# High and low halves of attention's output stored to two DRAM tensors, added there later by four DMAs; the third copy of q one tick later

## Chip, cores and metric

The kernel runs on one core of a Trainium2 chip. The metric is the device time of one execution in microseconds (us), lower is better. The engines are PE (TensorE, matmuls), ACT (ScalarE), DVE (VectorE), POOL (GpSimd) and SP (SyncE, which here only issues DMAs); sixteen DMA engines move data. DMAs that add to what they write (accumulating DMAs) are all issued by POOL in this kernel.

## What is computed

One decoder layer over 512 tokens and a width of 2048, float32. Attention is cut here to what the change touches:

```python
h = rms_norm(x, norm_gain[i])
z = h @ w_in[i]
q, k, v, g_attn, c_b, c_c, c_h, g_conv = jnp.split(z, SPLITS, axis=-1)
q = partial_rope(rms_norm(q, q_norm_gain[i]), pos)      # 16 heads of 64
k = partial_rope(rms_norm(k, k_norm_gain[i]), pos)      # 4 heads of 64
y_attn = sliding_window_attention(q, k, v, attn_sinks[i]) * jax.nn.silu(g_attn)   # window 128
y_conv = c_b * short_conv(c_c * c_h, conv_w[i]) * jax.nn.silu(g_conv)             # 3 taps
mix = jnp.concatenate([y_attn, y_conv], axis=-1)
x = x + mix @ w_out[i]
gate = jax.nn.sigmoid(rms_norm(x, ple_gate_norm_gain[i]) @ w_ple_gate[i] + b_ple_gate[i])
e = rms_norm(p[i] @ w_ple_proj[i], ple_norm_gain[i])
x = x + gate * e
```

## The kernel before

**Precision.** Every float32 operand of a matmul is split into a high part, which a cast rounds to PE's format, and a low part, the rest (`halves`, line 199 the cast on ACT, line 200 the subtraction on DVE). A product is three matmuls: high by high, low by high, high by low.

**Stages.** First the keys and values are projected (line 520). Then come nine *groups* of a Strassen-like product, groups 0 to 8, of 28 *steps* each; a step is 12 matmuls of 128x512 (line 241). Group 0 gives q. Between group 0 and group 1 stands the *attention stage*: it computes attention itself, together with the tiles of the convolution's input (`gemm_tile`, line 712) and the embedding's projection (line 900). Groups 1 to 3 go on with the convolution (`square_group`, `conv_group`), group 4 gates attention's output, groups 5 and 6 are the output projection, 7 and 8 the gate.

**What sets the order.** PE's order is written out by hand everywhere. In the groups the order of all other engines is by hand too: `soon(before, s, ...)` and `soon(after, s, ...)` enter work into tables that step s empties. In the attention stage only PE's is: there a scheduler orders ACT, DVE, SP and POOL, from the order in which the program issues the work and its own estimates. Each engine runs its own list in order and waits where an operand isn't there. The stage's program order is made of *ticks*: every six matmuls of `gemm_tile` call `tick`, which issues all that was entered by `at(when, ...)` up to that tick.

**Attention.** Sixteen *units* (j, n): key head j, in the order 2, 3, 0, 1, and block n of 128 queries. For a pair of blocks, `turn_q` (five ticks before the unit's scores) transposes q into PSUM (line 791), splits it into `st` and `low`, and builds the two tiles that the scores need with three copies of half a tile each, DMAs from SBUF to SBUF that POOL issues: line 795 `st2` upper half from `st`, 796 `st2` lower half from `low`, 797 `st` lower half from `low`. The third overwrites what the first reads, so it waits until the first has landed.

Per unit then: scores on PE (`pss`, lines 814 and 815), masking and maximum on DVE (823 to 831), four exponentials on ACT (line 833, tile `prob`); four ticks later `turn`: PE transposes `prob` (line 842, `pst`), ACT and DVE split it into `pth` and `ptl`, and POOL makes masked copies `pph` and `ppl` (line 849, affine select) of it; three ticks after that `values`: four matmuls into `pso` (line 859) with `pth`, `ptl`, `pph`, `ppl` in this order. The values' high and low parts lie side by side in the weights, so the upper 64 rows of the result `up` (line 861) are the high part's and the lower 64 the low part's; their sum is the output. The kernel forms that sum in DRAM: line 863 stores the upper half into `attn_dram[j]` (the tile `a`), and line 864, entered twelve ticks after the scores, adds the lower half with an accumulating DMA. That one reads and writes what 863 wrote, so POOL waits ahead of it until 863 has landed.

```python
rows = attn_dram[j].rearrange("(r d) (n t) -> d r n t", d=HD, n=NB)[:, :, n]
nc.gpsimd.dma_start(rows, up[:HD])
cell["add"] = lambda: nc.gpsimd.dma_start(rows, up[HD:], accum_op=ALU.add)
```

**After attention.** `attn_dram` is read in group 4 (line 1132, `load_raw`), from step 18 of that group on. Group 1's *taps* (line 1055 on DVE, its store line 1056 on POOL, tile `t`) run into the first steps of group 2: six products of the tile `z` with a row, each stored to DRAM. The fifth tap's product goes to the buffer from which the fourth tap's store still reads, so DVE waits for that store. POOL also issues the accumulating DMAs of the weights' sums (line 169, tile `wy`).

Of the kernel before, what the change touches and what calls it, by code (L numbers as in the profile page):

```python
# [9 lines left out]
F32 = mybir.dt.float32  # L10
F32R = mybir.dt.float32r
AF = mybir.ActivationFunctionType
ALU = mybir.AluOpType
E = mybir.EngineType

P = 128
T = 512
D = 2048
KT = D // P
NB = T // P  # L20
HD = 64
NH = 16
NKV = 4
# [12 lines left out]
def hymba_layer(ctx: ExitStack, tc: tile.TileContext, io):  # L36
# [14 lines left out]
    nc = tc.nc  # L51
# [5 lines left out]
    dram = ctx.enter_context(tc.tile_pool(name="dram", bufs=1, space=bass.MemoryType.DRAM))  # L57
# [54 lines left out]
    PER = len(steps) // NG  # L112
# [4 lines left out]
    before, after = {}, {}  # L117

    def soon(table, s, fn, *args):
        table.setdefault(s, []).append((fn, args))  # L120
# [3 lines left out]
    for g in range(NG):  # L124
        w, n = groups[g]
# [72 lines left out]
    def halves(h, l, src):  # L198
        nc.scalar.copy(h, src)  # L199
        tt(l, src, f32(h), op=ALU.subtract)  # L200
# [90 lines left out]
    def h_slot(home):  # L291
        return home, home_pool(home).tile([P, 2, 2 * P], F32R, tag=home, name="form")
# [44 lines left out]
        soon(before, s0 + 21, lambda: join(qs[1, 1], g, "a", ALU.subtract))  # L337
        soon(after, s0 + 26, lambda: join(qs[0, 0], g, "c", ALU.add))

    attn_dram = [dram.tile([2 * P, T], F32, name=f"a{j}") for j in range(NKV)]  # L340
    conv_dram = [dram.tile([P, T], F32, name=f"c{i}") for i in range(4)]
    mix_dram = [dram.tile([P, T], F32, name=f"m{i}") for i in range(8)]
    tap_dram = [dram.tile([T, T], F32, name=f"t{i}") for i in range(3)]
# [339 lines left out]
    def mtile(name):  # L683
        return misc.tile([P, T], F32, tag="m", name=name)
# [5 lines left out]
    def at(when, fn):  # L690
        later.append((when, len(later), fn))
# [91 lines left out]
    def turn_q(j, t):  # L783


        pt = ps_m.tile([P, T], F32, name="psm")
        for b in range(2):
            for f in range(2):
                s = j % 2 * 2 * P + f * P
                i = 2 * b + f  # L790
                nc.tensor.transpose(pt[:, i * P : (i + 1) * P], qs[t, j // 2][:, b, s : s + P], ident)
        st, st2 = (rowp.tile([P, T], F32R, tag="rows", name="st") for _ in range(2))
        low = misc.tile([P, T], F32R, tag="m", name="low")
        halves(st, low, pt)
        nc.gpsimd.dma_start(st2[:HD], st[HD:])
        nc.gpsimd.dma_start(st2[HD:], low[HD:])
        nc.gpsimd.dma_start(st[HD:], low[:HD])
        turned[j, t, 0], turned[j, t, 1] = st, st2

    turned = {}  # L800

    def attention(j, n, when):

        lo = 0 if n else P
        cell = {}
# [49 lines left out]
        def values():  # L855
            po = ps_o.tile([P, 4, P], F32, name="pso")
            for i, (w, x) in enumerate(cell["pt"]):
                w = w.rearrange("p s d -> p (s d)")
                nc.tensor.matmul(po, w, x, start=i == 0, stop=i == len(cell["pt"]) - 1)  # L859
            up = mtile("up").rearrange("p (r t) -> p r t", t=P)  # L860
            nc.scalar.copy(up, po)
            rows = attn_dram[j].rearrange("(r d) (n t) -> d r n t", d=HD, n=NB)[:, :, n]
            nc.gpsimd.dma_start(rows, up[:HD])
            cell["add"] = lambda: nc.gpsimd.dma_start(rows, up[HD:], accum_op=ALU.add)

        if n % 2 == 0:
            at(when - 5, lambda: turn_q(j, n // 2))
        at(when, scores)
        at(when + 4, turn)
        at(when + 7, values)  # L870
        at(when + 12, lambda: cell["add"]())


    pgs = []
# [31 lines left out]
    for u, (j, n) in enumerate(order):  # L906
        attention(j, n, 13 + 35 * u // 15)
# [101 lines left out]
    def new_pair(into, j, move=False):  # L1009
        raw = [spare("raw") for _ in range(2)]  # L1010
        into[j], work = make_forms(raw, lambda: spare("g"), form_slot, drop=let_go, move=(lambda: itile("g")) if move else None)
        pairs[id(into), j] = raw, work
# [116 lines left out]
    def load_raw(j, src):  # L1129
        new_pair(mixf, j, move=j == 4)  # L1130
        for i in range(2):
            nc.sync.dma_start(pairs[id(mixf), j][0][i], src[(2 * j + i) % 8])

    attn_tiles = [attn_dram[i // 2][i % 2 * P : (i % 2 + 1) * P] for i in range(8)]

    def attn_group(g):
# [24 lines left out]
        for j, when, plan in (  # L1161
# [4 lines left out]
        ):  # L1166
            soon(after, s0 + when, load_raw, j, mix_dram)
            for s, names in plan.items():
                soon(after, s0 + s, pieces, mixf, j, names)
# [266 lines left out]
    low = h_slot("fx")  # L1436
# [88 lines left out]
def build(arrays):  # L1525
    import concourse.bacc as bacc

    nc = bacc.Bacc("TRN2", target_bir_lowering=False, num_devices=1)
    io = {
        n: nc.dram_tensor(f"in_{n}", v.shape, mybir.dt.from_np(v.dtype), kind="ExternalInput").ap()  # L1530
        for n, v in arrays.items()
    }
    io["out"] = nc.dram_tensor("out_t", (NB, P, D), F32, kind="ExternalOutput").ap()
    with tile.TileContext(nc) as tc:
        hymba_layer(tc, io)
    return nc
# [9 lines left out]
```

## Time and profile before

| | |
|---|---|
| Runs shown (three) | 913.33, 914.39, 915.92 us; median 914.39 |
| The profiled execution | 912.85 us; its span, first to last instruction, 911.1 us |
| PE busy | 900.5 us, 99% of the span; granted clock 0.998 |
| DVE, ACT, POOL busy | 714.1, 527.7, 193.0 us (78%, 58%, 21%) |
| Attention stage | from about 127 to 280 us of the span |
| Groups 1 and 2 | from 280 to about 433 us |

All times below are us from the start of the span. A row of the timeline gives start, duration, engine, line, operation, its tiles as out<-in, and in brackets how long the engine was idle ahead of it and what ended the wait. A matmul's duration is its latency; PE starts one of 128x512 every 0.23 us, so back-to-back rows start 0.23 apart. A DMA's row on POOL is its issue; the transfer lands later. A wait that no engine on the path feels costs nothing: POOL is idle for most of the span.

### The profile page before, as it was taken

What the parts mean: (1) busy time and instruction counts of PE and PEld (TensorE: products, weight loads), DVE (VectorE), ACT (ScalarE), POOL (GpSimd) and SP (SyncE); (2) the same over time, 40 slices, a digit from 0 to 9 for tenths busy, and PEclk for the clock granted to TensorE, in tenths of its full rate; (3) what the DMA queues carried; (4) which work ended last, traced back from release to release, by engine and by line L of the source; (5) the groups of instructions that cost most, each with busy time, mean ns of one, the idle gap of its engine ahead of it and who ended that gap; (6) DMA issues with size and microseconds to landing.
All of it is one profiled execution on the core that took longest, in us unless ns stands there. A gap on an engine that the chain in (4) does not pass through costs nothing.

```text
span 911.1 us, 11967 instructions
## 1 busy us (share of the span) xinstructions
PE 900.5 (99%) x4130; PEld 746.3 (82%) x4130; DVE 714.1 (78%) x967; ACT 527.7 (58%) x849; POOL 193.0 (21%) x264
## 2 busy tenths in 40 slices
PE   9999999999999999999999999999999999999997
PEld 7888888887878888888888888888888888888885
DVE  6878889887757687877768678997858887799678
ACT  6766848676653443454344457766556666665453
POOL 4232143376640001100130110012120112111100
PEclk9999999999999999999999999999999999999999
DMA  8999558756668858648478897858996995898647
GB/s 312 360 292 308 212 61 274 246 112 133 151 130 310 288 173 237 179 147 257 126 201 247 222 237 257 234 127 230 341 293 198 212 293 142 234 306 256 185 139 219
DMA packets 74445, 202.34 MB, mean 222 GB/s; under 512 B 8867, under 2 KB 15331, under 8 KB 74384
## 3 DMA queue, kind: packets, MB, share of 16 engines
q1 hardware_dynamic: 48672, 134.24, 43.1%
q0 software_dynamic: 25568, 67.33, 33.0%
q8 instruction: 32, 0.52, 0.2%
q14 instruction: 29, 0.24, 0.1%
q10 hardware_dynamic: 144, 0.01, 0.0%
HBM read 166.94 MB, written 31.46 MB: 218 GB/s over the span
## 4 chain that ended last, share of the span: by engine, by line
PE 86%; DVE 5%; issue 2%; ACT 2%; DMA 2%; POOL 2%; SPq 0%; DVEq 0%; POOLq 0%; ACTq 0%
PE psp L241 68%; PE psg L712 4%; PE pst L241 4%; PE psp L520 3%; PE pst L1024 2%; PE pss L900 1%; PE pst L1422 1%; PE pst L900 1%; DMA raw<-in_w_kv 1%; DVE wl L200 1%; DVE z L1320 1%; PE pso L859 1%; DMA st<-st 1%; DVE ptl L200 0%; DMA a<-up 0%
## 5 line engine op out<-in xcount | busy, mean ns | idle before, releaser
L241 PE MATMUL psp<-wh,form 128*128 128x512 f32 x1280 | 395.3, 390 | 0.0
L241 PEld LDWEIGHTS psp<-wh,form 128*128 128x128 f32 x1280 | 239.4, 188 | 49.2
L241 PE MATMUL psp<-wl,form 128*128 128x512 f32 x640 | 249.4, 390 | 0.0
L200 DVE TENSOR_TENSOR wl<-wy,wh 128x1024 fp32r<-128x1024 f32 x108 | 131.5, 1221 | 58.6 <-ACT wh L199 57.9
L199 ACT CAST wh<-wy 128x1024 fp32r<-128x1024 f32 x108 | 113.4, 1051 | 91.6 <-PE psp L241 72.4
L241 PEld LDWEIGHTS psp<-wl,form 128*128 128x128 f32 x640 | 120.1, 188 | 25.8 <-DVE wl L200 0.8
L200 DVE TENSOR_TENSOR wl<-wx,wh 128x1024 fp32r<-128x1024 f32 x72 | 87.9, 1222 | 51.2 <-ACT wh L199 51.1
L199 ACT CAST wh<-ws 128x1024 fp32r<-128x1024 f32 x72 | 75.8, 1053 | 74.0 <-PE psp L241 53.0
L241 PE MATMUL psp<-wh,hsh 128*128 128x512 f32 x304 | 118.6, 390 | 0.0
L241 PE MATMUL psp<-wl,hsh 128*128 128x512 f32 x304 | 118.3, 389 | 0.0
L241 PE MATMUL psp<-wh,hsl 128*128 128x512 f32 x304 | 118.3, 389 | 0.0
L199 ACT CAST wh<-wx 128x1024 fp32r<-128x1024 f32 x72 | 75.6, 1052 | 70.9 <-PE psp L241 49.9
L200 DVE TENSOR_TENSOR wl<-ws,wh 128x1024 fp32r<-128x1024 f32 x72 | 88.0, 1222 | 29.2 <-ACT wh L199 28.9
L189 DVE TENSOR_TENSOR wy<-wy,ws 128x1024 f32<-128x1024 f32 x72 | 87.6, 1217 | 0.0
L241 PEld LDWEIGHTS psp<-wl,hsh 128*128 128x128 f32 x304 | 57.1, 188 | 11.9
L241 PEld LDWEIGHTS psp<-wh,hsl 128*128 128x128 f32 x304 | 57.1, 188 | 11.8
L241 PEld LDWEIGHTS psp<-wh,hsh 128*128 128x128 f32 x304 | 57.1, 188 | 11.7
L712 PE MATMUL psg<-hsh,wh 128*128 128x512 f32 x112 | 45.3, 405 | 0.0
L712 PE MATMUL psg<-hsh,wl 128*128 128x512 f32 x112 | 43.8, 391 | 0.0
L712 PE MATMUL psg<-hsl,wh 128*128 128x512 f32 x112 | 43.8, 391 | 0.0
L169 POOL DMA_DIRECT2D wy<-in_w_mid x16 | 14.0, 876 | 136.9 <-DVE wy L189 83.3
L199 ACT CAST wh<-raw 128x1024 fp32r<-128x1024 f32 (+1 forms) x29 | 29.1, 1005 | 19.7 <-DMA raw<-in_w_ple_proj 6.9
(236 smaller groups left out, 1332.1 us busy)
## 6 DMA issues: line engine op xcount, KB each, us to landing
ws<-in_w_mid SPq DMA_DIRECT2D x40, 512.0 KB, 4.5
wx<-in_w_mid SPq DMA_DIRECT2D x24, 512.0 KB, 4.4
wy<-in_w_mid SPq DMA_DIRECT2D x20, 512.0 KB, 6.1
h<-form POOLq DMA_DIRECT2D x32, 256.0 KB, 5.7
wy<-in_w_mid POOLq DMA_DIRECT2D x16, 512.0 KB, 8.8
raw<-in_w_in SPq DMA_DIRECT2D x16, 512.0 KB, 4.6
wx<-in_w_out SPq DMA_DIRECT2D x16, 512.0 KB, 6.7
ws<-in_w_out SPq DMA_DIRECT2D x16, 512.0 KB, 6.2
```

The costliest lines, as they stand in the source:

```text
L169: nc.gpsimd.dma_start(t, w[n, r, j, c], accum_op=ALU.add)
L189: tt(y, y, got[g, "s1" if f == 6 else "s0", c], op=ALU.add)
L199: nc.scalar.copy(h, src)
L200: tt(l, src, f32(h), op=ALU.subtract)
L241: nc.tensor.matmul(ps[t], a, w[:, i], start=start and first and i == 0 and n == 0, stop=last and i == 1 and n == 2, skip_group_check=not s ...
L520: nc.tensor.matmul(kv_ps[t // 2][:, t % 2], hs[k][a][:, t * P : (t + 1) * P], kv_split[c][w][:, i], start=k == 0 and n == 0, stop=k == KT ...
L712: nc.tensor.matmul(ps, w[:, k % 8], a, start=k == 0 and n == 0, stop=k == KT - 1 and n == 2)
L859: nc.tensor.matmul(po, w, x, start=i == 0, stop=i == len(cell["pt"]) - 1)
L900: nc.tensor.matmul(banks[t], a, w[:, k], start=k == 0 and i == 0, stop=k == 1 and i == 2)
L1024: nc.tensor.transpose(pt[:, b], quads[b // 2][:, b % 2, f * P : (f + 1) * P], ident)
L1320: stt(z[:, b, cols], z[:, b, cols], column(r_e, t, b), ext[t, n][b][:, cols], op0=ALU.mult, op1=ALU.mult)
L1422: nc.tensor.matmul(ps, w[:, k % 8], a, start=k == 0 and n == 0, stop=k == KT - 1 and n == 2)
```

## The change

- `low_dram` is new: four DRAM tensors `l`, shaped as `attn_dram`. `values` issues two plain stores in a row (both on line 864 now), the upper half of `up` to `a`, the lower half to `l`. The sixteen accumulating DMAs of line 864 and their entries at `when + 12` are gone.
- `add_low` (line 1135) adds the whole of `low_dram[j]`, 512 KB, to `attn_dram[j]` with one accumulating DMA from DRAM to DRAM, in rows of 128 numbers. The four are entered after steps 4, 9, 14 and 19 of group 2.
- `turn_q` returns its third copy (now line 798) in place of issuing it; it is entered one tick later, at `when - 4`.

```diff
-    attn_dram = [dram.tile([2 * P, T], F32, name=f"a{j}") for j in range(NKV)]
+    attn_dram, low_dram = ([dram.tile([2 * P, T], F32, name=f"{x}{j}") for j in range(NKV)] for x in "al")
...
         nc.gpsimd.dma_start(st2[:HD], st[HD:])
         nc.gpsimd.dma_start(st2[HD:], low[HD:])
-        nc.gpsimd.dma_start(st[HD:], low[:HD])
         turned[j, t, 0], turned[j, t, 1] = st, st2
+        return lambda: nc.gpsimd.dma_start(st[HD:], low[:HD])
...
-            rows = attn_dram[j].rearrange("(r d) (n t) -> d r n t", d=HD, n=NB)[:, :, n]
-            nc.gpsimd.dma_start(rows, up[:HD])
-            cell["add"] = lambda: nc.gpsimd.dma_start(rows, up[HD:], accum_op=ALU.add)
+            for i, x in enumerate((attn_dram, low_dram)):
+                rows = x[j].rearrange("(r d) (n t) -> d r n t", d=HD, n=NB)[:, :, n]
+                nc.gpsimd.dma_start(rows, up[i * HD : (i + 1) * HD])
 
         if n % 2 == 0:
-            at(when - 5, lambda: turn_q(j, n // 2))
+            at(when - 5, lambda: cell.update(last=turn_q(j, n // 2)))
+            at(when - 4, lambda: cell["last"]())
         at(when, scores)
         at(when + 4, turn)
         at(when + 7, values)
-        at(when + 12, lambda: cell["add"]())
...
+    def add_low(j):
+        nc.gpsimd.dma_start(attn_dram[j], low_dram[j], accum_op=ALU.add, max_dma_last_dim=T)
+
+    for j in range(NKV):
+        soon(after, 2 * PER + 4 + 5 * j, add_low, j)
```

The lists of PE, DVE, ACT and SP hold the same instructions in the same order as before; only POOL's differs, from the 69th instruction on. Three places of it follow; a row is line, operation and tiles.

The first place is on POOL about the middle of the attention stage, from the three copies for units (0, 0) and (0, 1) on. Before:

```order
L795 DMA st<-st 64x512
L796 DMA st<-low 64x512
L797 DMA st<-low 64x512
L863 DMA a_85<-up 64x4x128
L849 AFFINE_SELECT pph<-pth 128x512
L864 DMA a_85<-up 64x4x128
L849 AFFINE_SELECT ppl<-ptl 128x512
L863 DMA a_86<-up 64x4x128
```

The same place of POOL's list in the change:

```order
L795 DMA st<-st 64x512
L796 DMA st<-low 64x512
L798 DMA st<-low 64x512
L864 DMA a_85<-up 64x4x128
L864 DMA l_89<-up 64x4x128
L849 AFFINE_SELECT pph<-pth 128x512
L864 DMA a_86<-up 64x4x128
L849 AFFINE_SELECT ppl<-ptl 128x512
```

Between `pph` and `ppl` stood an accumulating store that waits for the store two rows above it; now a plain store of the next unit stands there, and the pair of stores comes ahead of `pph`. The third copy stands where it stood, directly behind the other two.

The second place is on POOL at the end of the attention stage, the last units (1, 2) and (1, 3) and the first accumulating DMAs of group 1. Before:

```order
L849 AFFINE_SELECT pph<-pth 128x512
L863 DMA a_84<-up 64x4x128
L849 AFFINE_SELECT ppl<-ptl 128x512
L864 DMA a_84<-up 64x4x128
L863 DMA a_84<-up 64x4x128
L849 AFFINE_SELECT pph<-pth 128x512
L849 AFFINE_SELECT ppl<-ptl 128x512
```

In the change:

```order
L849 AFFINE_SELECT pph<-pth 128x512
L864 DMA a_84<-up 64x4x128
L849 AFFINE_SELECT ppl<-ptl 128x512
L864 DMA l_88<-up 64x4x128
L864 DMA a_84<-up 64x4x128
L864 DMA l_88<-up 64x4x128
L849 AFFINE_SELECT pph<-pth 128x512
```

Ahead of the last `pph` there was one accumulating store and one plain one; now there are three plain ones, none of which waits for another's landing.

The third place is on POOL in groups 1 and 2, the taps' stores (line 1056). One piece of the difference, from the third tap's store on, before and in the change:

```order
L1056 DMA t_99<-z 128x2x512
L1056 DMA t_101<-z 128x2x512
L1056 DMA t_100<-z 128x2x512
L1056 DMA t_99<-z 128x2x512
L169 DMA wy<-in_w_mid 128x1024 x4
```

```order
L1056 DMA t_103<-z 128x2x512
L1135 DMA a_83<-l_87 1024x128
L1056 DMA t_105<-z 128x2x512
L1056 DMA t_104<-z 128x2x512
L1135 DMA a_84<-l_88 1024x128
L1056 DMA t_103<-z 128x2x512
L1135 DMA a_85<-l_89 1024x128
L1135 DMA a_86<-l_90 1024x128
L169 DMA wy<-in_w_mid 128x1024 x4
```

The first addition stands ahead of the fourth tap's store, the second ahead of the sixth, and the last two behind the sixth, ahead of group 3's weight sums. Each waits on POOL only for the stores of the attention stage, so it is issued when POOL reaches it.

## The prediction

> **What bounds the kernel now.** I read the page first, then the busy time by stage, then PE's waits, then POOL's groups in the attention stage, and at the waits the timelines of PE, POOL, ACT and DVE.
>
> ```profile
> span 911.1 us, 11967 instructions
> PE 900.5 (99%) x4130; PEld 746.3 (82%) x4130; DVE 714.1 (78%) x967; ACT 527.7 (58%) x849; POOL 193.0 (21%) x264
> ...
> 270.00:560.00 290.00, 290.00 (x1297) 240.39 (x1296) 215.15 (x206) 132.69 (x141) 32.11 (x41) 1.00 0.74 219
> ```
>
> PE is idle for 911.1 - 900.5 = 10.6 us of the span, and in groups 1 to 3 (the third row, 270 to 560 us) for none. The change adds no matmul and takes none away, so all that it can win is idle time of PE, and all that it can lose is new idle time. PE's waits by releaser tell how much of it the touched instructions cause:
>
> ```profile
> PE pso L859 <- POOL ppl L849: 1.8, 1, 1.8
> ...
> PE pso L859 <- POOL pph L849: 0.6, 1, 0.6
> PE pss L814 <- DMA st<-low: 0.4, 1, 0.4
> ```
>
> Three waits, all in the attention stage, 2.8 us: for `ppl`, for `pph`, and for the third copy of q. Against this stand POOL's own waits there (the groups of 166 to 290 us; after the bar busy time, mean ns, then idle time and its releasers):
>
> ```profile
> L864 POOL DMA_DIRECT2D a<-up x16 | 17.0, 1089 | 25.6 <-DMA a<-up 24.3 <-PE pss L815 1.4
> ...
> L797 POOL DMA_DIRECT2D st<-low x7 | 4.3, 617 | 8.1 <-DMA st<-st 7.2 <-DVE rope L413 0.7 <-issue 0.2
> ```
>
> POOL waits 24.3 us in all for a store ahead of the accumulating stores that follow it. These are gone with the change, but they are not the gain: POOL is off the path, and PE feels two of them. The gain is read at those two.
>
> **First place: `ppl` at 211.** POOL's rows, DVE's for `ptl`, and PE's (unit (3, 1)):
>
> ```profile
> 205.64 0.65 POOL L863 DMA_DIRECT2D a<-up  x1
> 206.29 0.66 POOL L849 TENSOR_SCALAR_AFFINE_SELECT pph<-pth 128x512 fp32r<-128x512 f32 x1
> 209.82 1.06 POOL L864 DMA_DIRECT2D a<-up  x1 [2.87 <-DMA a<-up]
> 210.49 1.05 POOL L849 TENSOR_SCALAR_AFFINE_SELECT ppl<-ptl 128x512 fp32r<-128x512 f32 x1
> ...
> 205.97 0.69 DVE L200 TENSOR_TENSOR ptl<-pst,pth 128x512 fp32r<-128x512 f32 x1
> ...
> 209.43 0.39 PE L859 MATMUL pso<-pph,vd 128*128 128x512 f32 x1
> 211.59 0.50 PE L859 MATMUL pso<-ppl,vd 128*128 128x512 f32 x1 [1.78 <-POOL ppl L849]
> ```
>
> `ptl` is there at 206.66, but `ppl` stands behind the accumulating store, which waits for the landing of the store at 205.64, and ends at 211.54. PE would have come to it at 209.43 + 0.23 = 209.66 and starts at 211.59: **1.93 us** lost. In the change two plain stores of 0.65 stand ahead of `pph` and one between `pph` and `ppl`. Even if the third copy again goes out as late as before (it ends at 205.64 there), `pph` ends at 205.64 + 2 x 0.65 + 0.66 = 207.6 and `ppl` at 207.6 + 0.65 + 0.66 = 208.9, ahead of 209.66. The wait goes whole.
>
> What is late next? PE goes on to the transposes of (3, 2), whose last exponential is long done (first row), so it runs on. ACT and DVE can't follow at once: ACT is in the exponentials of (3, 3), which depend on scores from before the wait, until 210.66 + 0.48 = 211.14, and after those come the copy `up` and `pth`:
>
> ```profile
> 207.66 0.48 ACT L833 ACTIVATE prob<-prob,negms,msq 128x128 f32<-128x128 f32 x1
> 210.66 0.48 ACT L833 ACTIVATE prob<-prob,negms,msq 128x128 f32<-128x128 f32 x1
> 212.62 0.59 ACT L199 CAST pth<-pst 128x512 fp32r<-128x512 f32 x1
> ...
> 213.50 0.69 DVE L200 TENSOR_TENSOR ptl<-pst,pth 128x512 fp32r<-128x512 f32 x1
> ...
> 231.87 0.48 ACT L833 ACTIVATE prob<-prob,negms,msq 128x128 f32<-128x128 f32 x1
> ...
> 233.43 0.60 PE L791 MATMUL psm<-ident,z 128*128 128x128 f32 x4
> ...
> 184.59 0.48 ACT L833 ACTIVATE prob<-prob,negms,msq 128x128 f32<-128x128 f32 x1
> ...
> 185.30 0.48 PE L712 MATMUL psg<-hsh,wh 128*128 128x512 f32 x1
> ```
>
> So `pth` moves from 212.62 to 211.14 + 0.1 + 0.48 (the copy) = about 211.7, and `ptl`, which waits for it, from 213.50 to 211.7 + 0.59 + 0.05 = 212.35: DVE moves by 1.15 us, not by 1.93. I let DVE keep that lag (a gap in its work would shorten it). The first place where the lag could reach PE is the transposes of (0, 2): their last exponential ends at 231.87 + 0.48 = 232.35, and PE's next work begins at 233.43. At 184.6 PE did wait for exponentials, and went on 185.30 - (184.59 + 0.48) = 0.23 us after the last. Moved by 1.15, the exponentials let PE go on at 232.35 - 1.15 + 0.23 = 231.43; PE, moved by 1.93, comes at 231.50. It fits by 0.07 us: this place lets through 2.0 us and no more. Of the first gain I take 1.93.
>
> **The third copy.** PE's wait for it is worth 0.4 us in the row above. In the change it still stands directly behind the first two and still waits for the first one's landing; what it is spared is queueing behind accumulating stores. It comes ahead of `pph` now, which has 0.8 us to spare by the sum above. If its 0.4 us goes, it goes before the place that lets 2.0 through, so it is worth at most 2.0 - 1.93 = 0.07. I take 0; the ends are 0 and 0.4.
>
> **Second place: the last unit.** POOL, PE, ACT and DVE:
>
> ```profile
> 264.34 1.06 POOL L864 DMA_DIRECT2D a<-up  x1 [3.83 <-DMA a<-up]
> ...
> 265.76 0.39 PE L859 MATMUL pso<-ptl,vv 128*128 128x512 f32 x1
> 266.75 0.49 PE L859 MATMUL pso<-pph,vd 128*128 128x512 f32 x1 [0.60 <-POOL pph L849]
> ...
> 267.67 0.40 PE L712 MATMUL psg<-hsh,wh 128*128 128x512 f32 x1
> ...
> 262.04 0.58 ACT L861 COPY up<-pso 128x512 f32<-128x512 f32 x1
> 262.52 0.58 ACT L199 CAST pth<-pst 128x512 fp32r<-128x512 f32 x1
> ...
> 263.31 0.68 DVE L200 TENSOR_TENSOR ptl<-pst,pth 128x512 fp32r<-128x512 f32 x1
> ```
>
> Without a wait PE reaches its next tile at 265.76 + 3 x 0.23 = 266.45; it does so at 267.67: **1.22 us** lost, since `pph` and `ppl` stand behind a store that waited 3.83 us. In the change `pph` has two plain stores ahead of it that need `up` (262.62) and nothing else: 262.62 + 1.3 + 0.66 = 264.6, `ppl` 265.2, where PE wants them at 265.99 and 266.22. All four engines move together here, for the chain of this unit starts at PE's scores, so the distance holds. Nothing is late next: PE goes on with matmuls whose operands are loaded.
>
> **The four additions.** They take no time of PE, ACT or DVE. The size that matters is D, the time the DMA engines need for one. From 211.25 to 212.45 (1.2 us) one accumulating store of 512-byte rows has the engines to itself; the other rows are the page's 512 KB accumulations into SBUF and 128 KB stores of `up`, the taps' stores, two rows of DVE, and a piece of the chain that ended last:
>
> ```profile
> q0 software_dynamic: 230, 0.12, 100.3%
> ...
> wy<-in_w_mid POOLq DMA_DIRECT2D x16, 512.0 KB, 8.8
> ...
> a<-up POOLq DMA_DIRECT2D x32, 128.0 KB, 3.4
> ...
> DMA to landing us min/median/max: 3.2/3.8/7.4
> ...
> 365.96 0.75 POOL L1056 DMA_DIRECT2D t<-z  x1 [0.61 <-DVE z L1055]
> 373.18 0.75 POOL L1056 DMA_DIRECT2D t<-z  x1 [6.46 <-DVE z L1055]
> ...
> 381.19 1.22 DVE L1055 TENSOR_TENSOR z<-z,tap 128x1024 f32<-128x1024 f32 x1
> ...
> 385.73 1.22 DVE L200 TENSOR_TENSOR wl<-wy,wh 128x1024 fp32r<-128x1024 f32 x1
> ...
> 280.09 160.48 PE psp L241 x708
> ```
>
> One packet takes 16 x 1.2 x 1.003 / 230 = 84 ns of an engine. An addition is 1024 packets of that size, 64 for each engine: D = 5.4 us. No row shows DRAM to DRAM. Above I bound it by the 8.8 us in which a 512 KB accumulation from DRAM lands, waits included; below by the 3.2 us of a plain 512 KB store (the row of `t`, which gives 3.2 to 7.4). I take 5.4, the row of the same packet size.
>
> Behind the first addition on POOL's queue stands the fourth tap's store, issued at 373.18; for that store waits DVE's fifth tap, 381.19; behind it on DVE stand the splits of weights. The third tap's store, the slowest of the six, lands at 365.96 + 7.4 = 373.4. The addition follows in the same queue, then the fourth store with about 1.6 us of its own: it lands at 373.4 + D + 1.6 = 380.4, ahead of 381.19. If it is later, PE feels nothing until the split at 385.73 is 2.4 us late: it feeds step 12 of group 2, which starts 40 steps of 160.48 / 59 = 2.72 us after 280.09, at 388.9, and its third matmul needs the low part 0.45 later; the split ends at 386.95. So PE waits only from D = 381.19 - 375.0 + 2.4 = **8.6 us** on, then one for one; at the upper bound 0.2 us. The other three additions have the weights of later steps beside them and only the sixth tap's store behind them, which no engine waits for soon. POOL spends at least 1.06 us (256 rows) and at most 4 times that on issuing one: between the third store's issue and 373.18 it has 6.5 us idle. In the attention stage it saves 0.4 us for each of sixteen stores (1.06 against 0.65).
>
> A rule speaks against this. The row of DMA traffic for 366 to 379 us:
>
> ```profile
> q1 hardware_dynamic: 9, 0.04, 1.5%
> ```
>
> The queue of the weight loads takes 1.5% of the engines there. By the Trainium skill, DMA: Bandwidth & Descriptors, section Queues, rings and completion order, each DMA engine takes turns between the queues that have work. By that rule a full weight queue would leave an addition half of each engine, and the time would be that of rival 5; by the row there is next to nothing to take turns with at the first addition, and the sum stays. The trace so far shows no addition beside a full weight queue.
>
> **Sum.** 1.93 + 0 + 1.22 = 3.15 us. The profiled execution took 912.85 us, 1.75 more than its span, so it becomes 909.7. It lies 1.54 below the median of the runs shown, 914.39; the time I predict is the median's, 914.39 - 3.15 = **911.2 us**, faster by 0.34%. About 0.3%, 2.7 us, is what a measurement of this kernel can tell from no change.
>
> **Rivals.**
> 1. *The exponentials take the wait's place.* If ACT and DVE don't move at all after 211, PE can pass (0, 2) only 0.23 after 232.35, at 232.58 in place of 233.43: 0.85 us of the first gain is left, 0.85 + 1.22 = 2.07, 912.3 us. For it: a fit by 0.07 us is no margin. Against: `pth` and `ptl` have only the copy ahead of them.
> 2. *All three waits go whole*, 0.4 + 1.93 + 1.22 = 3.55: 910.8 us. Against it stands the 2.0 at (0, 2).
> 3. *The change doesn't unblock POOL.* The third copy, 7.2 us of waits, now stands ahead of `pph`; if its landing wait grows by over 0.8 us, `ppl` is late again and only the last unit gains: 1.22, 913.2 us. For it: the order. Against: fewer slow stores in the queue.
> 4. *Slower: the first addition holds the fourth tap's store.* If rows from DRAM to DRAM cost much more than 84 ns, DVE stands at the fifth tap and PE runs dry at step 12. It decides from D = 8.6; the gain is eaten at D = 8.6 + 3.15 = 11.75. With each quarter taking the whole 3.4 us in which such a 128 KB store lands (the page's median), D = 13.6, a loss of 5.0: 916.2 us; at twice that, 930.
> 5. *The first addition shares the engines with weight loads.* If loads came as it runs and each queue had half, D would be 2 x 5.4 = 10.8, a loss of 2.2: 913.4 us. Against: the 1.5%.
>
> **How the numbers follow.** Forecast 0.50, rival 1 0.21, rival 2 0.08, rival 3 0.07, rival 4 0.11, rival 5 0.03. Faster by over 0.3% means below 911.65. Runs of one kernel lie about 1 us apart, so of the forecast seven in ten fall there, all of rival 2 and a tenth of rival 1: 0.35 + 0.08 + 0.02 = 0.45. Rival 4 lies beyond +0.3% in most of its span: 0.09. The rest, 0.46, is within. The range takes in the forecast, rivals 1 to 3 and 5, the bounds of D and half a us of the runs' spread on either side: 910.0 to 914.2; rival 4 is left out.
>
> **What would show it.** Right: POOL's groups have no wait for `a<-up`; PE's waits for `ppl` and `pph` are gone; the transposes of (0, 2) start without a wait or with one under 0.3 us; idle time of PE in the attention stage near 0; an addition lands within 9 us and DVE's fifth tap has no wait. Wrong: a wait of `pst` for `prob` near 1 us (rival 1); `ppl` still a releaser of PE (rival 3); the fifth tap waiting for `t<-z` and PE idle in group 2 (rival 4). The forecast also falls if PE turns out to be paced by something hidden in its modelled ends.

## The result, and the profile after

| | Runs | Median (lowest to highest), us | Ratio to before, 95% interval |
|---|---|---|---|
| before | 6 | 914.66 (912.13 to 915.92) | |
| changed | 6 | **909.65** (909.37 to 910.13) | 0.9949 (0.9935 to 0.9964) |
| before, a second set | 29 | 913.83 (911.40 to 916.49) | |
| changed, the same set | 12 | 910.13 (909.46 to 914.04) | 0.9961 (0.9946 to 0.9975) |

The ratios, which are those of the means, make the kernel faster by 3.6 to 4.7 us; the medians lie 5.0 and 3.7 us apart. The changed kernel's runs lie closer together: all of its eighteen but one are within 1.5 us. The profiled execution went from 912.85 to 909.53 us, by 3.32.

The head of the page after:

```profile
span 907.8 us, 11971 instructions
...
PE 898.9 (99%) x4130; PEld 746.0 (82%) x4130; DVE 714.2 (79%) x967; ACT 527.7 (58%) x849; POOL 193.0 (21%) x268
```

The row of groups 1 to 3 in its busy times by stage:

```profile
270.00:560.00 290.00, 290.00 (x1297) 240.44 (x1296) 216.76 (x209) 135.45 (x147) 36.18 (x43) 1.00 0.79 226
```

PE is idle for 8.9 us in place of 10.6, and in groups 1 to 3, where the additions run, still for none. PE's waits by releaser have one row of the attention stage left, and POOL's groups there have no wait for a landing of `a`:

```profile
PE pso L859 <- POOL ppl L849: 0.6, 1, 0.6
```

```profile
L864 POOL DMA_DIRECT2D a<-up x16 | 10.2, 637 | 17.9 <-ACT up L861 16.7 <-issue 1.0
L864 POOL DMA_DIRECT2D l<-up x16 | 10.1, 631 | 1.1 <-issue 1.1
...
L798 POOL DMA_DIRECT2D st<-low x7 | 3.7, 527 | 6.5 <-DMA st<-st 6.5
```

The first place, POOL and then PE:

```profile
205.99 0.62 POOL L864 DMA_DIRECT2D a<-up  x1
206.61 0.65 POOL L849 TENSOR_SCALAR_AFFINE_SELECT ppl<-ptl 128x512 fp32r<-128x512 f32 x1
...
208.80 0.39 PE L859 MATMUL pso<-pph,vd 128*128 128x512 f32 x1
209.03 0.39 PE L859 MATMUL pso<-ppl,vd 128*128 128x512 f32 x1
```

`ppl` ends at 207.26, 1.8 us ahead of its matmul, which follows the one before it by 0.23. The second place reads the same: the four matmuls of the last `pso` start 0.23 apart and the next tile 0.23 behind them. What is left is at unit (0, 2). POOL, DVE and PE there:

```profile
231.07 0.65 POOL L864 DMA_DIRECT2D l<-up  x1 [1.07 <-issue]
231.73 0.65 POOL L849 TENSOR_SCALAR_AFFINE_SELECT pph<-pth 128x512 fp32r<-128x512 f32 x1
232.32 1.71 POOL L849 TENSOR_SCALAR_AFFINE_SELECT ppl<-ptl 128x512 fp32r<-128x512 f32 x1
...
232.33 1.21 DVE L200 TENSOR_TENSOR wl<-raw,wh 128x1024 fp32r<-128x1024 f32 x1
...
234.08 0.50 PE L859 MATMUL pso<-ppl,vd 128*128 128x512 f32 x1 [0.63 <-POOL ppl L849]
```

`ppl` took 1.71 us here in place of 0.65, beside a split of weights on DVE, and PE lost time that it did not lose before. The two other profiles with the same order here (`changed_again`, `no_additions`) have the same 1.71.

Set against the same matmuls of before, PE is 0.7 us earlier by 100 us (ahead of anything that the change touches), gains 0.57 at the third copy, gives back 0.66 at the transposes of (3, 1) right behind it, gains 2.0 at the first place, gives back 0.9 at (0, 2), gains 1.2 at the last unit, and 0.3 at the end. The attention stage gives 2.3 of the 3.3 us.

The additions, POOL's rows and DVE's fifth tap:

```profile
361.70 0.75 POOL L1056 DMA_DIRECT2D t<-z  x1 [0.62 <-DVE z L1055]
362.44 1.41 POOL L1135 DMA_DIRECT2D a<-l  x1
368.86 0.79 POOL L1056 DMA_DIRECT2D t<-z  x1 [5.01 <-DVE z L1055]
...
378.17 1.22 DVE L1055 TENSOR_TENSOR z<-z,tap 128x1024 f32<-128x1024 f32 x1
```

The issue of an addition takes 1.4 us. The first one lands 11.3 us after its issue began, 4.0 us behind the third tap's store ahead of it, and the fifth tap does not wait.

### The profile page after: what moved, and what is told of

Its sections match the earlier page's. It is cut to its first block, busy times and chain, and to the rows that moved or that the text cites. A ratio compares the mean times of both kernels' runs of the same rounds, so it can differ in the third digit from the quotient of the medians.

```text
span 907.8 us, 11971 instructions
## 1 busy us (share of the span) xinstructions
PE 898.9 (99%) x4130; PEld 746.0 (82%) x4130; DVE 714.2 (79%) x967; ACT 527.7 (58%) x849; POOL 193.0 (21%) x268
## 4 chain that ended last, share of the span: by engine, by line
PE 72%; DVE 3%; ACT 2%; issue 1%; DMA 1%; POOL 0%; DVEq 0%; ACTq 0%; POOLq 0%
PE psp L241 60%; PE psg L712 4%; PE pst L241 4%; PE pst L1024 2%; PE pst L1428 1%; PE pso L859 1%; ACT prob L833 1%; DVE z L1326 1%; DVE wl L200 0%; PE pst L842 0%; DMA wx<-in_w_out 0%; PE pss L815 0%; PE pss L814 0%; DMA st<-st 0%; DVE wy L189 0%
## 5 line engine op out<-in xcount | busy, mean ns | idle before, releaser
L833 ACT ACTIVATE prob<-prob,negms,msq 128x128 f32<-128x128 f32 x64 | 30.8, 483 | 16.9 <-DVE negms L831 16.9
```

Source lines behind the costliest of these rows:

```text
L833: nc.scalar.activation(t[:, r], t[:, r], AF.Exp, scale=r_q[:, r : r + 1], bias=negm[:, r : r + 1], accum_out=sums[:, r : r + 1],)
```

## The experiments

Two things had to be explained: how the change gains more than the one profile of before showed as waits, and why the runs of before lie so far apart. In a diff, `...` marks lines left out. "Lists" are the instructions of each engine in order.

### Parts of the change

**Only the third copy later** (`copy_only`).

```diff
-        nc.gpsimd.dma_start(st[HD:], low[:HD])
         turned[j, t, 0], turned[j, t, 1] = st, st2
+        return lambda: nc.gpsimd.dma_start(st[HD:], low[:HD])
...
-            at(when - 5, lambda: turn_q(j, n // 2))
+            at(when - 5, lambda: cell.update(last=turn_q(j, n // 2)))
+            at(when - 4, lambda: cell["last"]())
```

> The kernel before with only the third copy entered a tick later. The lists of all five engines hold the same instructions in the same order as before, so this is also a second look at the kernel before. Every theory: ratio 1.000 within 0.002, runs between 912 and 916 us. Its profile is a second execution to read: if it lies above 914 us (the profile of before lay at 912.85), the place where it is later than that profile names the loss that the median of before has and its profile doesn't show. Theory A (landings of the accumulating stores vary, POOL hands the delay to pph and ppl): more than three PE waits for pph or ppl, in the attention stage. Theory B (the weight loads for group 1 wait for the buffers from which the last accumulating stores read): PE idle at 280 to 295 us. Theory C (launch, head or tail): PE's starts differ before 127 us or after 820 us.

914.86 us (911.42 to 919.32, 12 runs), ratio 1.0012 (0.9991 to 1.0032): no effect that shows. The profile, at 911.42 us, has the same lists as before and no wait at 211. So the wait that carried most of my sum is not a property of the program: it comes in some executions.

**The changed kernel without that edit** (`split_copy_early`): the two hunks above undone in the changed kernel.

> The changed kernel with the third copy issued in the program where it was before. In the lists one low store of POOL changes places with the affine select behind it, nothing else. All theories: the time of the changed kernel, 909.6 us within 0.5; the tick of the third copy has no part in the gain. Rival: the copy's tick is worth the 0.4 us that PE waited for it: 910.0.

910.32 us (909.68 to 913.47, 9 runs), ratio 0.9956 (0.9940 to 0.9972). The median is 0.2 to 0.3 us above both forecasts, but the interval is that of the changed kernel: no part of the gain that could be told apart belongs to the tick.

The profile is of the slowest of these nine runs, 913.47 us, and shows a loss that lies far from the change. PE's waits at a split of weights (all three between 805 and 822 us), and ACT's row ahead of them:

```profile
PE psp L241 <- DVE wl L200: 1.7, 3, 1.1
```

```profile
803.24 1.05 ACT L199 CAST wh<-wx 128x1024 fp32r<-128x1024 f32 x1 [5.26 <-DMA wx<-in_w_ple_gate]
```

A load of weights came late, the splits behind it too, and PE waited three times. By the starts of the same matmuls this execution is 1.0 us behind the changed kernel's profile at 790 us and 3.9 us behind it at 825. Why the load was late stays open. It is not tied to the accumulating stores of attention: this kernel has none.

**Without the additions** (`no_additions`).

```diff
-    for j in range(NKV):
-        soon(after, 2 * PER + 4 + 5 * j, add_low, j)
```

> The changed kernel without the four additions from DRAM to DRAM; the low part of attention's output is left out. If the additions are hidden, as the prediction has it, the time is that of the changed kernel, 909.65 us within 0.3, and PE's idle time is the same 8.9 us. Rival: they hold transfers or POOL's queue somewhere after 360 us without a wait of PE that the one profile shows: then 0.5 to 1.5 us less.

910.46 us (909.57 to 911.14, 7 runs), ratio 0.9964 (0.9949 to 0.9978). The median is 0.5 us above the end of the forecast, and the interval is that of the changed kernel in the second set: leaving the additions out saves nothing that can be measured.

**Two stores for some key heads alone** (`split_231`, `split_1`): with a list of heads for which the change is made; the others keep the accumulating store at `when + 12`.

```diff
+    SPLIT = (0, 2, 3)
...
             for i, x in enumerate((attn_dram, low_dram)):
+                if i and j not in SPLIT:
+                    rows = attn_dram[j].rearrange("(r d) (n t) -> d r n t", d=HD, n=NB)[:, :, n]
+                    cell["add"] = lambda: nc.gpsimd.dma_start(rows, up[HD:], accum_op=ALU.add)
+                    break
```

> Two stores and a later addition for key heads 2, 3 and 0 alone; key head 1, the last four units, as before. The profile's sum: the wait for ppl at 211 goes (1.9 us less 0.9 given back at (0, 2)), the last unit's 1.1 stays: 1.0 us, 913.7 by the medians. Theory A (varying landings of accumulating stores all over the stage): three quarters of the extra 1.4 us too, about 2.1 us, 912.5, spread about 1.5. Theory B (loads for group 1 behind the last accumulating stores): no more than the profile's 1.0, and the spread of 3 to 4 us stays.

> Two stores and a later addition for key head 1 alone, the last four units; the other heads as before. The profile's sum: the last unit's wait goes, 1.1 us, the one at 211 stays: 913.5 by the medians. Theory A: a quarter of the extra 1.4 us besides, about 1.5 us, 913.2, spread about 3. Theory B: all of the extra, 2.5 us or more, 912.1 or less, and the spread shrinks below 1.5 us.

Heads 2, 3, 0: 911.83 us (911.02 to 915.02), ratio 0.9978 (0.9964 to 0.9992). Head 1 alone: 912.54 us (909.82 to 914.69), ratio 0.9984 (0.9967 to 1.0001), in two groups of six runs, 909.8 to 911.5 and 913.6 to 914.7. Against before's 914.51 in that set their medians gain 2.7 and 2.0 us, together the whole change; the interval of the second just takes in no gain. Both medians gain more than the profile's sum for their part. Neither theory's pair of numbers was met: theory A asked for 2.1 and 1.5, theory B for no more than 1.0 in the first. No profile has PE idle at the start of group 1 either; the busy row of the kernel before in a late execution (`before_p5`, below):

```profile
276.00:300.00 24.00, 24.00 (x107) 19.87 (x107) 18.75 (x18) 8.87 (x10) 0.62 (x2) 1.00 0.95 341
```

### The landing or the adding

The prediction's reason was the wait for the first store's landing. An accumulating store differs in a second way: it takes longer itself, on POOL and until it lands.

**Waits kept, adding gone** (`overwrite`, `overwrite_again`).

```diff
-            cell["add"] = lambda: nc.gpsimd.dma_start(rows, up[HD:], accum_op=ALU.add)
+            cell["add"] = lambda: nc.gpsimd.dma_start(rows, up[HD:])
```

> The kernel before with the sixteen second stores plain: each overwrites the first store's rows where it added to them, so the high part of attention's output is left out. Same lists on all engines, same waits of POOL for the first store's landing; only the adding is gone. Wait theory (the loss and its spread come from POOL standing behind the landing, wherever the landing is late): as before, 914.5 us, runs 3 us or more apart. Adding theory (an accumulating store is itself slow, in issue on POOL, 1.06 against 0.65 us, or in landing): most of the 4.7 us goes, 910 to 911.5, runs within 1.5 us.

> The overwriting kernel again, on the same chip as the one with two copies: 909.4 us within 0.6, runs within 1.5 us but for one or two; below the kernel before by 3.5 to 5.2 us.

909.40 us (908.74 to 912.06), ratio 0.9943 (0.9922 to 0.9963); again 909.41 (908.78 to 910.76), 0.9940 (0.9922 to 0.9959). The wait theory, by which nothing should have changed, falls: the whole gain is there although every second store still has to wait for the first one's landing. POOL's group, and the median time from issue to landing of these stores, which was 3.4 us before:

```profile
L864 POOL DMA_DIRECT2D a<-up x16 | 10.2, 637 | 22.7 <-DMA a<-up 18.9 <-PE pso L859 2.8 <-PE pss L815 0.7
```

```profile
a<-up POOLq DMA_DIRECT2D x32, 128.0 KB, 2.5
```

POOL still waits 18.9 us for `a<-up`, against 24.3 before, and by PE's waits none of that reaches PE. What differs is the adding: a second store takes 637 ns of POOL in place of 1089, 0.45 us less at each of the sixteen, and the stores land sooner.

**Adding kept, waits gone** (`add_no_wait`, `add_no_wait_2`; in the second the early transfers stand at steps 22 and 23).

```diff
+    for j in range(NKV):
+        soon(after, 18, lambda j=j: nc.gpsimd.dma_start(low_dram[j], io["x"][2 * j : 2 * j + 2].rearrange("k p t -> (k p) t")))
...
-                nc.gpsimd.dma_start(rows, up[i * HD : (i + 1) * HD])
+                nc.gpsimd.dma_start(rows, up[i * HD : (i + 1) * HD], **({"accum_op": ALU.add} if i else {}))
```

> The changed kernel with the sixteen low stores accumulating again, into tensors that four early transfers at 100 to 110 us filled with a part of x, so that no wait for a landing comes with them; the output has that part of x added. Wait theory: as the changed kernel, 909.7 to 910.5 us (POOL 0.4 us longer at each store, some of it felt), runs within 1.5 us. Adding theory: back towards before, 912 to 914.5, with a spread of 3 us.

> As the last kernel with accumulating low stores and no landing waits, but its four early transfers stand three to five steps later, about 111 to 116 us, where the DMA engines are nearly idle, so that they don't make PE wait for weights; the output has a part of x added. Adding theory: 913 to 915 us with runs 3 us apart (the last one's 917.7 less the 3.6 us that its early transfers cost PE at 96 to 103 us). Wait theory: 909.5 to 910.5.

The first, 917.69 us (915.21 to 919.71), ratio 1.0034 (1.0021 to 1.0047), can't be read: its early transfers made PE wait for weights, and by the starts of the same matmuls it is 3.6 us later at 103 us already. The second has no such wait: 912.07 us (911.50 to 913.79), ratio 0.9980 (0.9968 to 0.9992), between the two forecasts. Its PE waits in the attention stage are now mostly for `pph`:

```profile
PE pso L861 <- POOL pph L851: 2.2, 2, 1.4
```

Together, by medians:

| us | POOL waits for the landing | it doesn't |
|---|---|---|
| second store plain | 909.4 (`overwrite`) | 909.65, 910.13 (changed) |
| second store adds | 913.8 to 915.1 (before) | 912.07 (`add_no_wait_2`) |

The wait alone costs nothing, the adding alone about 2 us, both together 3.7 to 5.7, with the wide spread. So both are needed for the whole loss: without the adding all of it goes, without the wait 1.8 us (913.83 less 912.07).

### POOL's time or the transfer

**Copies on POOL in place of the adding** (`pool_filler`; `pool_filler_2` with two copies in place of four), on top of the overwriting kernel. `pad` is a tile that nothing uses.

```diff
-            cell["add"] = lambda: nc.gpsimd.dma_start(rows, up[HD:], accum_op=ALU.add)
+            def second():
+                nc.gpsimd.dma_start(rows, up[HD:])
+                for i in range(4):
+                    nc.gpsimd.tensor_copy(pad[HD:], up[HD:, i, :32])
+            cell["add"] = second
```

> The overwriting kernel (both stores plain, same waits for landings as before; the high part is left out) with four small copies on POOL behind each second store, about 0.4 us of POOL's time, what an accumulating store takes more than a plain one. Theory POOL time (an accumulating store costs because POOL, in order, reaches pph and ppl 0.4 us later each time): most of the loss comes back, 912.5 to 914.5 us, runs 3 us apart. Theory transfer (it costs in the queue's transfers, where reading, adding and writing takes longer and what stands behind it lands late): as the overwriting kernel, 909.4 to 910.3.

> The overwriting kernel (the high part is left out) with two small copies on POOL behind each second store in place of four, about 0.5 us of POOL's time where four took 1.0 and an accumulating store takes 0.42 more than a plain one. Theory POOL time alone: half of the 7.1 us that four copies cost, 3.5 us, 912.9 us, within 1 us of the kernel before, whose remaining loss then is small. Theory POOL time and late landings together: less than half, 910.5 to 912, the kernel before 2 us or more above it.

Four copies: 916.48 us (915.43 to 920.11), ratio 1.0028 (1.0017 to 1.0040), 2 us above the highest forecast; they took about 1.0 us of POOL and not the 0.4 that was planned. Two: 915.29 us (913.03 to 918.99), ratio 1.0007 (0.9990 to 1.0024), above the times of both forecasts. About half a us of POOL at each second store, without any adding, is enough to bring back the time of the kernel before and its spread (911.37 to 917.93 in that set). That POOL's time is all that acts in the kernel before is not shown by it: there the adding makes landings late as well (below).

The size is not in proportion, though: 0.5 us costs 5.9 (915.29 less 909.41), and 1.0 us costs 7.1 (916.48 less 909.40). The two profiles show part of the reason. Four copies, a row of POOL's timeline and PE's waits:

```profile
206.96 1.03 POOL L867 COPY pad<-up 64x32 f32<-64x32 f32 x4
```

```profile
PE pso L859 <- POOL ppl L849: 4.8, 6, 1.2
```

Six waits, none over 1.2 us. Two copies, profiled at 917.27 us, the same two views, and PE's rows around its one long wait:

```profile
207.50 0.50 POOL L867 COPY pad<-up 64x32 f32<-64x32 f32 x2
```

```profile
212.85 0.50 PE L859 MATMUL pso<-ppl,vd 128*128 128x512 f32 x1 [2.31 <-POOL ppl L849]
213.19 1.01 PE L842 MATMUL pst<-ident,prob 128*128 128x128 f32 x4
...
216.78 0.40 PE L712 MATMUL psg<-hsl,wh 128*128 128x512 f32 x1
```

Busy times of the same execution in steps of 1 us (sum, then PE, PEld, DVE, ACT, POOL; then PE's granted clock, DMA share, GB/s):

```profile
214.00:215.00 1.00, 1.00 (x7) 1.00 (x6) 0.00 (x0) 0.59 (x1) 0.00 (x0) 0.50 0.59 115
215.00:216.00 1.00, 1.00 (x6) 1.00 (x6) 0.90 (x5) 0.00 (x0) 0.55 (x1) 0.50 0.00 0
```

After PE has stood for 2.31 us its clock is halved, from 213.2 to 216.6. From the transposes to the same matmul of the next tile it takes 216.78 - 213.19 = 3.59 us. This is one execution, 2 us slower than the median of its kernel. By the starts of the same matmuls it is 8.0 us behind `overwrite`'s profile; 4.2 us of that come at this place, and another 1.9 between 800 and 820 us, at a late load of weights as in `split_copy_early`.

### The kernel before again

**More profiles of it** (`before_again`, `before_p3` to `before_p6`; `copy_only` has its lists too).

> The kernel before once more, for another profile of it. Runs of it lie in clusters about 3 us apart (911.6 to 913, 914.3 to 916.5, over 917.5). If this profile lies in the second cluster, it shows the stall: wait theory, PE waiting about 3 us more in all for pph or ppl between 160 and 270 us, behind an accumulating store of POOL that waits; rival (weight loads behind the stores' buffers): PE idle at 280 to 295 us.

> The kernel before, for a profile of one of its slower executions (its runs go from 911.4 to 918.6 us, and the three profiles of its lists so far lie at 911.45, 912.85 and 913.17). If this one lies above 914: theory POOL time says that PE's waits for pph, ppl and the q copies between 190 and 270 us are together 2 us or more longer than in the profile at 911.45, each behind an accumulating store or a copy that landed late behind one. Rival (weight loads behind the buffers of the last accumulating stores): PE idle between 280 and 300 us. Rival (noise elsewhere): PE's starts differ before 127 us or after 300 us.

> As the last one: another profile of the kernel before, for a slower execution of it.

> As the last one: another profile of the kernel before, for a slower execution of it.

> As the last one: another profile of the kernel before, for a slower execution of it.

None took over 914 us; all seven lie below the medians of before (913.8 to 915.1), so what an execution at the median or above loses is on no profile. But the seven differ at the first place, all with the same lists. The third copy's delay is from the start of the first copy's issue to the start of its own; PE's idle time is 163 us less its busy time between 127 and 290 us:

| Profile | Execution, us | Third copy's delay | PE's wait for `ppl` at 211 | PE idle, 127 to 290 |
|---|---|---|---|---|
| before_again | 913.17 | 3.52 | 0.37 | 3.28 |
| copy_only | 911.42 | 4.37 | 0 | 1.30 |
| before_p3 | 913.62 | 4.38 | 0 | 2.05 |
| before_p4 | 911.94 | 4.41 | 0 | 1.63 |
| before_p6 | 912.43 | 4.57 | 0.50 | 2.35 |
| before | 912.85 | 5.12 | 1.78 | 3.02 |
| before_p5 | 913.42 | 5.84 | 2.15 | 3.70 |
| changed | 909.53 | | 0 | 1.06 |
| overwrite | 909.32 | | 0 | 0.17 |

In six of the seven the execution is the longer, the longer PE is idle between 127 and 290 us. The seventh, `before_p3`, has 2.05 us and the longest time: it waits 1.2 us at 821 us for weights, as `split_copy_early` does.

The third copy waits for the first one's landing, and that one stands in POOL's queue directly behind an accumulating store. It lands 3.2 to 5.6 us after the start of its issue in these seven; in the overwriting kernel, behind a plain store, after 2.4, and in the kernels with two and four copies after 3.4 and 2.7. So the copy lands 0.8 to 3.2 us later with the adding: at this place that is mostly more than the 0.45 us of POOL. The latest of the seven, POOL and PE:

```profile
200.19 1.00 POOL L795 DMA_DIRECT2D st<-st  x1
...
206.03 0.51 POOL L797 DMA_DIRECT2D st<-low  x1 [3.41 <-DMA st<-st]
...
211.07 1.05 POOL L849 TENSOR_SCALAR_AFFINE_SELECT ppl<-ptl 128x512 fp32r<-128x512 f32 x1
...
212.17 0.50 PE L859 MATMUL pso<-ppl,vd 128*128 128x512 f32 x1 [2.15 <-POOL ppl L849]
212.50 0.60 PE L842 MATMUL pst<-ident,prob 128*128 128x128 f32 x4
...
214.48 0.39 PE L712 MATMUL psg<-hsl,wh 128*128 128x512 f32 x1
```

The overwriting kernel, the same place on POOL:

```profile
202.34 0.52 POOL L797 DMA_DIRECT2D st<-low  x1
203.35 0.65 POOL L863 DMA_DIRECT2D a<-up  x1 [0.50 <-ACT up L861]
...
206.12 0.65 POOL L864 DMA_DIRECT2D a<-up  x1 [0.20 <-issue]
206.77 0.65 POOL L849 TENSOR_SCALAR_AFFINE_SELECT ppl<-ptl 128x512 fp32r<-128x512 f32 x1
```

There the third copy goes out without a wait, and `ppl` ends at 207.42, 1.6 us ahead of its matmul (209.04): a landing that much later is swallowed. Before, the chain of copy, store, wait, accumulating store and `ppl` had no such margin, and what a landing was late went to PE: 0 to 2.15 us in these seven.

In `before_p5`, after 2.15 us, the clock stays whole (the row of its busy times in steps):

```profile
213.00:214.00 1.00, 1.00 (x11) 1.00 (x11) 0.36 (x3) 0.78 (x2) 0.00 (x0) 1.00 0.71 162
```

The stretch that took 3.59 us with two copies takes 214.48 - 212.50 = 1.98. So between the wait of 2.15 and that of 2.31 us lies another 1.6. This may give the groups of runs some 3 us apart their shape: where the landing is late beyond that point, an execution would pay the wait and the slow stretch behind it. For the kernel before itself that is not shown. It was seen in one execution of the kernel with two copies, and of all profiles here that is the only one with a halved clock between 24 and 880 us. A rival is on record: the late loads of weights at 800 to 825 us cost up to 2.9 us in an execution (`split_copy_early`), with and without the accumulating stores. The one late run of a changed kernel that has a profile (913.47) shows them, and they are a part of before's spread too (`before_p3`). Which of the two makes the groups stays open.

### A version without POOL

**Both stores issued by ACT** (`stores_on_act`), on top of the change.

```diff
-                nc.gpsimd.dma_start(rows, up[i * HD : (i + 1) * HD])
+                nc.scalar.dma_start(rows, up[i * HD : (i + 1) * HD])
```

> The changed kernel with both stores of a unit issued by ACT, behind its copy up, in place of POOL: POOL's 32 issues of 0.63 us (20 us) go. PE's last wait for ppl in the changed kernel, 0.6 us, and what POOL's queue costs it besides should go: 909.0 to 909.5. Rival: the issue takes ACT's time and delays the exponentials: 910.5 or more.

The changed kernel beside it (`changed_again`, the second set of the table above):

> The changed kernel once more, on the same chip as the others of this set: 909.6 to 910.4 us, runs within 1.5 us but for one or two.

909.71 us (909.07 to 910.09, 5 runs), ratio 0.9952 (0.9936 to 0.9967), against the changed kernel's 910.13 and 0.9961. That is above the forecast and below the rival. By its waits PE has none left in the attention stage. The intervals overlap: whether it beats the change isn't told apart.

## Why the prediction was wrong, by its steps

The forecast was 911.2 us, the range began at 910.0, and the time is 909.65. The direction was right, and the sum for the profiled execution (909.7) came within 0.2 us of what was profiled (909.53). That nearness is partly luck: 1.0 of the 3.3 us came at the head and the end of the program, which the change doesn't touch, and the attention stage gave 2.3 against my 3.15. Rival 2 less half a us is 910.3 and not the 910.0 with which the range begins; the time is below either.

- **What bounds the kernel.** Right: only idle time of PE counted, and it was in the attention stage.
- **First place, 1.93 us, goes whole.** In the profile it did. As a price of the kernel before it was wrong: the same lists give 0 to 2.15 us there.
- **What is late next.** The limit of 2.0 us at (0, 2) by the exponentials didn't bind. The 0.9 us was given back at the same unit by another mechanism, a slow `ppl` on POOL.
- **Third copy, 0.** Right in size, wrong in place: its gain was given back 2 us later, at the transposes of (3, 1).
- **Second place, 1.22.** Measured 1.2.
- **Additions, no cost.** Right, though the first landed 11.3 us after its issue and not within 9. It stood behind the third tap's store, and landed 4.0 us behind it, where D was put at 5.4; the fourth tap's store still landed in time.
- **"In the attention stage it saves 0.4 us for each of sixteen stores."** This is the step of the mechanism that failed. I wrote the adding's cost down and put it at nothing, because POOL is idle for most of the span, and gave the whole gain to the waits for the landing ("these are gone with the change"). The runs show that the adding decides: without it, with the second stores still behind the landing, the gain is whole (`overwrite`, 4.4 and 5.7 us by the medians), and without the waits, with the adding, it is 1.8 (`add_no_wait_2`). The adding acts in two ways, both at nothing in my sum: 0.45 us of POOL at each store, of which half a us of copies is enough to lose the gain (`pool_filler_2`), and late landings, 4.8 in place of 2.4 us for the copy behind one at the first place. POOL works in order, and between a landing and `ppl` its time is on the path. How the loss divides between the two stays open.
- **"The time I predict is the median's, 914.39 - 3.15."** This is the step that put the number out of the range; by the profile alone it was 909.7. The sum from one execution was taken off the median of others, and the chances took runs to lie about 1 us apart, though before's three already lay 2.6 us apart. Before's median is 1.8 us above its profile (914.66 against 912.85), that of the changed kernel 0.1 (909.65 against 909.53), so the median had more to lose than that profile: 5.0 us in this set, 3.7 in the second. The adding is what makes the difference, since without it the median is down at 909.4 too; the place where an execution at the median of before loses it is on no profile.
- **Rivals.** None came. The first was near in place and size, 0.9 us given back at (0, 2), but not by exponentials. Not all three waits went whole without something given back (2). The third copy's wait did not grow (6.5 against 7.2 us), and the additions neither made the fifth tap wait (4) nor shared engines with loads to an effect (5).

## What to carry to other kernels

Where PE waits for a short job that stands in order behind a DMA's landing on another engine, take several profiles, and count every part of a us that the engine spends between the landing and the job, even if it is idle for four fifths of the span. Ask also what makes the landing late: here a copy landed after 3.2 to 5.6 us behind an accumulating store, and after 2.4 behind a plain one. Where the runs of a kernel spread wider than the difference to be explained, the waits of one profile can't stand for the median: here they added up to 3.15 us, and the medians lay 3.7 to 5.0 us apart. In one execution a wait of PE of 2.31 us cost 1.6 us more behind it.

## What the runs showed of the hardware that wasn't expected

- **The clock after a gap.** Behind a gap of 2.15 us PE's granted clock stayed at 1.00 (`before_p5`); behind one of 2.31 us it was 0.50 for some 3.4 us (`pool_filler_2`), one case of each. The Trainium skill, TensorE: Matmul & The Clock Gate, section HAM oscillation — how this bites in real kernels, has the half clock follow from gaps of more than about 3.4 us. The half is as measured; the gap that was enough here is shorter, and the measurement decides.
- **An accumulating store on POOL.** It lasts 1.03 to 1.13 us, or 1.45 directly behind another, against 0.62 to 0.70 for a plain one. Yet the next instruction's row starts 0.67 behind it, as behind a plain one, and lasts 0.4 longer in its turn. The Trainium skill, Perfetto Trace Analysis, section GPSIMD Engine Instruction, advises to time POOL by the distance of starts; by that the adding would cost nothing. Here the ends are what counts: `ppl` at 210.49 with 1.05 us ends at 211.54, and its matmul starts at 211.59.
- **POOL beside DVE.** The affine select of 0.65 us took 1.71 beside a subtraction of 128x1024 from SBUF on DVE (1.21 us). The Trainium skill, SBUF — State Buffer, section Who interferes with whom, says that a DVE instruction with two inputs in SBUF contends with one of GpSimd that reads SBUF; this row agrees. Two more profiles (`changed_again`, `no_additions`) have the same row, and beside a subtraction `ptl`, one input of which is in PSUM, the select takes 0.63 us.
